# A streaming-encoder block in f32: ten 8 KB tiles instead of nine, 22 slots of 4 KB instead of 24, and another place for the eight value pieces

## The chip, the cores and the metric

The kernel runs on one core of one Trainium2 chip. The metric is the device time of one execution in microseconds (us). The kernel before takes 2405.63 us, the median of three runs (2405.38 to 2405.67).

The engines go by the names of the profile: PE (TensorE, matmuls and transposes), DVE (VectorE), ACT (ScalarE), POOL (GpSimd) and SP (SyncE). Each works through its own queue of instructions in order. SP does nothing but start loads. POOL starts other DMAs, among them those that add to what they write.

## The reference

One layer of an encoder block over 256 tokens with 2048 features, in float32, with 256 memory tokens:

```python
x = x + 0.5 * swiglu(rms_norm(x, ffn1_norm), ffn1_w_up, ffn1_w_down)   # d_ff = 5632

h = rms_norm(x, mix_norm)
proj = h @ w_in                                  # 6144 + 4096 columns
q_a, f_a, i_a, g_a, x_b, gate_b, gates = jnp.split(proj, splits, axis=-1)
o_a = hgrn2_chunked(q_a, f_a, i_a, lb)           # 8 heads of 128; i_a are the values
y_a = rms_norm(o_a, hgrn_norm) * silu(g_a)
y_b = rglru_branch(x_b, gate_b, conv_w, conv_b, lru_wa, lru_ba, lru_wx, lru_bx, lru_lambda)
g = sigmoid(gates + b_gate)
x = x + (g[A] * (y_a @ w_branch_a) + g[B] * (y_b @ w_branch_b)) @ w_out

q, k, v = rms_norm(x, xattn_norm) @ wq, *split(rms_norm(mem, mem_norm) @ wkv)   # 4 heads of 512
x = x + (softmax(q @ k.T / sqrt(512)) @ v) @ wo

x = x + 0.5 * swiglu(rms_norm(x, ffn2_norm), ffn2_w_up, ffn2_w_down)
return rms_norm(x, final_norm)
```

## The kernel before

**Numbers in two parts.** Every weight comes from HBM in pieces of 128 x 2048 f32, 1 MB or 8 KB in each partition. ACT rounds a piece to PE's faster type, which gives `h`; DVE subtracts `h` from the raw piece, which gives the remainder `l` (function `split`, L556: ACT `h<-raw`, DVE `l<-raw,h`). Activations are split in the same way: `ops` (the operands of the projections, the high and the low part side by side in one tile), `xf`, `xh` and `xl` (x as it enters the feed-forwards), `hidop` (the hidden layer). PE makes three of the four products, high by high, high by low and low by high, into one PSUM bank `acc`.

**Four kinds of pieces** (function `prepare`, L664). A *plain* piece is a load (`raw`), one `h` and one `l`. A *fast* piece belongs to a product that is made with seven sub-products instead of eight, and needs sums of its quarters besides: DVE makes three differences into the tile `td`, and `td` is split as well, into `th` and `tl`. A *value* piece (kind `"seven"`, the weights `wv` of the values `i_a`) is of the same sort; its operands on the other side are sums of quarters of the activations, made by DVE in slots `xs` (function `sums_of`) and split into slots `xd`. A *made* piece has its sums worked out long ahead, between the two feed-forwards: POOL loads the weights into a tile `made` (`made<-wu`), DVE makes the differences in place (`made<-made`), POOL writes the tile out to DRAM (`kept<-made`), and in the second feed-forward SP loads it back (`td<-kept`). Besides these, an *added* piece has its `l` made by DMAs on POOL, in tiles `own` and `l`.

**Two rings of tiles in SBUF.** All tiles of 8 KB (`raw`, `h`, `l`, `td`, `tl`, `made`, `own` and others, function `big`) share one ring: nine places in the whole program, and four more within each feed-forward (`FFN_POOLS = dict(more=4)`, L836). The tiles of 4 KB (function `slot`) share a ring of 24: halves of the sums (`th`), `xs`, `xd`, `ops`, the silu, gate and score tiles, the biases of the gates (`bgate`), the probabilities and values of the attention. A tile can be written when the last reader of the tile that had its place before is through.

**The stages.** The head takes the memory's norm and its values (weights `wvm`) between the first pieces of the first feed-forward; the residual x comes twice, as `xin` (by tokens, tiles `x`) and as `xT` (by features, eight parts of 128 x 512 into the tile `xf`). Then come the first feed-forward (weights `wu`, `wd`), the projections `win` (40 pieces, one bank each) with the eight value pieces among the first twelve, the two recurrences as side work between the projections, the gates (`wg`, 32 pieces in eight groups; for each two groups one load of biases `bgate` on SP), the branches, the output, the attention (per head: scores, a softmax whose probabilities are `p`, transposes `acc<-vt,p` on PE), and the second feed-forward, which ends with the last norm (`to_out`). Each projection is 16 matmuls of 512 columns with `h` (`acc<-ops,h` or `acc<-h,ops`, by which operand is the stationary one) and 16 of 256 columns with `l` (`acc<-ops,l`); then ACT copies half of the bank (`lo`), and DVE adds and scales (`sum`, `silu`). Each value piece is 21 matmuls of 512 columns into seven banks, which stay open from the first value piece to the last. There are eight banks.

**Where the value pieces stand.** The program's units of work for the first half are four `unit_f`, four `unit_silu(Q)` and four `unit_silu(G)`, twelve projections. Entry `a` of a list of eight numbers puts one value piece ahead of projection number `a` (numbered from 0; 12 is the end). The list stands twice for the weights' plan and once for the units:

```python
after = [2, 4, 5, 7, 8, 9, 11, 12]
more = [f for n in range(13) for f in [lambda: next(vs)] * after.count(n) + more[n:n + 1]] + [lambda: next(vs)]
```

**What sets the order.** The code doesn't issue its instructions directly. Each call is recorded (`Flow.record`, L220), and at the end a planner (`Flow.arrange`, L286) simulates the five queues with prices of its own (`Flow.price`), gives each operation a due time from the PE work that needs it (`aims`), and takes for each queue, of the operations whose inputs are ready, the one that is due first, if the ring has a place. So the number of places in a ring decides how far ahead a load or a `split` may be put. For the shared ring, the place is refused while earlier-due operations still lack theirs; for the slots, `fit` keeps a number of places spare, set by `3 if bufs == 24 else ...` (L173). The order is then written out by one loop (L488, which is why almost all rows of the profile show L488), with the semaphores that the order needs. All of PE's 11579 matmuls and transposes and all other operations are the same whatever the order; what differs is which stands ahead of which.

Of the kernel before, what the change touches and what calls it, by code (L numbers as in the profile page):

```python
# [80 lines left out]
class View:  # L81


    def __init__(self, tile, cells, steps=()):
        self.tile, self.cells, self.steps = tile, cells, steps
# [77 lines left out]
class Pool:  # L163
# [5 lines left out]
    def tile(self, shape, dt, name, tag=None, bufs=None):  # L169
        tag = tag or name  # L170
        if tag not in self.rings:
            bufs = bufs or self.bufs
            self.rings[tag] = Ring(tag, 3 if bufs == 24 else bufs // 4 if bufs >= 8 else bufs)  # L173
            self.rings[tag].extend(self, bufs)
        return Buffer(self.rings[tag], shape, dt, name, self.scope, "space" in self.kw)

# [23 lines left out]
class Flow:  # L200
# [22 lines left out]
    def pool(self, name, bufs, scope=None, **kw):  # L223
        self.pools.append(Pool(self, name, bufs, scope, **kw))
        return self.pools[-1]
# [267 lines left out]
def block_kernel(tc: tile.TileContext, xT, xin, memT, mem, vec, gfin, bgate, lruw, wu1, wd1, win, wv,  # L493
                 wg, wab, wout, wq, wk, wvm, wo, wu2, wd2, out_):
    flow = Flow(tc)
    pe, dve, act, sp, gps = flow.queues
    pool = flow.pool

    const = pool("const", 1)
    flow.share("big", pool("big", 9), 9)  # L500

    def big(name, dt=F32R):
        return flow.shared("big", [P, 2048], dt, name)

    slots = pool("slots", 24)
    small = pool("small", 2)
    dram = pool("dram", 1, space=bass.MemoryType.DRAM)
    psum = pool("psum", 8, space=bass.MemoryType.PSUM)
# [70 lines left out]
    def plan_columns(name, w, which):  # L579
        plan.extend(((name, i), w[i], "plain") for i in which)  # L580
# [6 lines left out]
    for hf in range(2):  # L587
        order = [*range(8 + hf * 4, 12 + hf * 4), *range(hf * 4, hf * 4 + 4), *range(16 + hf * 4, 20 + hf * 4)]
        for n, i in enumerate(order):
            for p, a in enumerate([2, 4, 5, 7, 8, 9, 11, 12] if hf == 0 else ()):  # L590
                if a == n:
                    plan.append((("v", "seven", p), wv[p], "seven"))
            plan_columns("in", win, [i])
        for p, a in enumerate([2, 4, 5, 7, 8, 9, 11, 12] if hf == 0 else ()):
            if a == 12:
                plan.append((("v", "seven", p), wv[p], "seven"))
    for hf in range(2):
# [285 lines left out]
    def turned_half(tile, y):  # L883

        acc = bank()
        for m in (2 * y, 2 * y + 1):
            for t in range(2):
                pe.transpose(acc[:, m % 2 * T + t * P:][:, :P], tile[:, t * 512 + m * P:][:, :P], ident)
        return acc
# [422 lines left out]
    def unit_silu(to, base, i):  # L1312
        hf, h = divmod(i, 4)
        if h == 0:
            to[hf] = slot(name="silu")
        s = summed(proj(base + i), by=rs["f"])
        o = heads(to[hf])[:, h]
        act.activation(o, s, ACT.Sigmoid)
        dve.tensor_tensor(out=o, in0=o, in1=s, op=ALU.mult)

    def unit_f(i):
        hf, h = divmod(i, 4)
        if h == 0:
            F[hf] = slot(name="f")
        s = summed(proj(8 + i), by=rs["f"])
        o = heads(F[hf])[:, h]
        act.activation(s, s, ACT.Sigmoid)
        dve.tensor_scalar(out=o, in0=s, scalar1=oml[:, i:i + 1], scalar2=lb[:, i:i + 1], op0=ALU.mult, op1=ALU.add)
# [9 lines left out]
    def units_v():  # L1338
        both = Halves()

        def sums(p):
            return sums_of([xg2[p // 2][:, p % 2 * 512 + j * P:][:, :P] for j in range(4)], both.new("xs"))

        accs = {}
        yield from seven("v", xs, sums, accs)
        joined(accs, [v[t][:, c * 512:(c + 1) * 512] for t in range(2) for c in range(2)])
        for t in range(2):
            act.activation(v[t], v[t], ACT.Copy, scale=rs["t"][:, t:t + 1])
        yield
# [171 lines left out]
    for hf in range(2):  # L1521
        more = [lambda i=i: unit_f(i) for i in range(hf * 4, hf * 4 + 4)]
        more += [lambda i=i: unit_silu(Q, 0, i) for i in range(hf * 4, hf * 4 + 4)]
        more += [lambda i=i: unit_silu(G, 16, i) for i in range(hf * 4, hf * 4 + 4)]
        if hf == 0:
            vs = units_v()
            after = [2, 4, 5, 7, 8, 9, 11, 12]
            more = [f for n in range(13) for f in [lambda: next(vs)] * after.count(n) + more[n:n + 1]] + [lambda: next(vs)]
        units += more
        units += [lambda hf=hf: side.append(hgrn(hf)) or True]  # L1530
# [291 lines left out]
```

## Time and profile before

| | |
|---|---|
| median of three runs | 2405.63 us (2405.38 to 2405.67) |
| the profiled execution | 2406.53 us, span in the profile 2404.8 us |
| busy: PE, DVE, ACT, POOL | 2392.7 (99%), 2128.1 (88%), 1473.3 (61%), 91.8 (4%) us |
| granted TensorE clock, mean | 0.999 |
| HBM | 581.12 MB read, 62.91 MB written, 268 GB/s over the span |

The profile was taken in one execution of its own, 0.90 us longer than the median of the runs; its span leaves out 1.7 us around the instructions. A row of a wait (`PE acc L488 <- DVE p L488: 1.4, 1, 1.4`) names the engine that stood still, the tile it was to write, who released it, the sum of the idle time in us, how often, and the longest. A row of the timeline gives the start in us, the time busy, the engine and the group of instructions, and in brackets the idle time just before with its releaser. In a row of windows stand, for one stretch, the busy time and the number of instructions of PE, PEld, DVE, ACT and POOL, then the granted clock, the busy share of the DMA engines and GB/s. In a row of instruction groups stand the busy time in us and the mean of one in ns, then the idle time of the engine in front of them. `x` and a number behind a group is how many instructions it holds; the names of x's tiles end in numbers (`x_304`).

### The profile page before, as it was taken

How to read it: one execution, taken by the hardware profiler on the slowest of the kernel's cores; microseconds unless marked ns; L12 is line 12 of the kernel's file. 1: busy time of each engine (PE TensorE's matmuls, PEld its weight loads, DVE VectorE, ACT ScalarE, POOL GpSimd, SP SyncE). 2: the span in 40 equal slices, each digit the busy share in tenths (PEclk: the TensorE clock that was granted, in tenths of full speed). 3: DMA queues.
4: the chain of work that ended last, by engine and by line, in shares of the span. 5: the costliest groups of instructions: out<-in, count | busy, mean ns of one | idle time of the engine just before them, and what ended most of it. 6: DMA issues, size and time to landing. Idle time of an engine off the chain costs nothing. (4 is left out here: it accounts for less than half of the span.)

```text
span 2404.8 us, 31100 instructions
## 1 busy us (share of the span) xinstructions
PE 2392.7 (99%) x12078; PEld 2000.9 (83%) x12078; DVE 2128.1 (88%) x2350; ACT 1473.3 (61%) x1470; POOL 91.8 (4%) x153
## 2 busy tenths in 40 slices
PE   9999999999999999999999999999999999999998
PEld 8888888888888888888888888888888888888887
DVE  7899999999996999888977788878799999999995
ACT  8767666666676655435773354555676666666663
POOL 0000000000000000000000000000000000000000
PEclk9999999999999999999999999999999999999999
DMA  9677788877776688889889899886898777777763
GB/s 370 238 261 243 258 261 263 262 256 253 260 252 204 224 321 297 322 306 347 315 312 338 316 371 363 305 303 248 309 378 319 262 262 262 263 262 262 259 265 114
DMA packets 101813, 678.58 MB, mean 282 GB/s; under 512 B 11296, under 2 KB 12064, under 8 KB 27296
## 3 DMA queue, kind: packets, MB, share of 16 engines
q1 hardware_dynamic: 79776, 523.40, 57.9%
q0 software_dynamic: 21168, 152.05, 20.1%
q8 instruction: 95, 1.56, 0.2%
q10 hardware_dynamic: 720, 1.13, 0.1%
q14 instruction: 54, 0.44, 0.1%
HBM read 581.12 MB, written 62.91 MB: 268 GB/s over the span
## 5 line engine op out<-in xcount | busy, mean ns | idle before, releaser
L488 DVE TENSOR_TENSOR l<-raw,h 128x2048 fp32r<-128x2048 f32 (+2 forms) x421 | 846.7, 2013 | 135.7 <-ACT h L488 62.3
L488 ACT ACTIVATE h<-raw 128x2048 fp32r<-128x2048 f32 (+2 forms) x421 | 711.1, 1693 | 391.5 <-PE acc L488 176.9
L488 PE MATMUL acc<-h,xh 128*128 128x512 f32 x1238 | 481.7, 390 | 0.3 <-DVE ev L488 0.3
L488 PE MATMUL acc<-h,xl 128*128 128x512 f32 x1238 | 481.6, 389 | 0.0
L488 ACT ACTIVATE h<-td 128x1024 fp32r<-128x1024 f32 (+1 forms) x264 | 326.0, 1241 | 200.3 <-DVE td L488 163.5
L488 DVE TENSOR_TENSOR tl<-td,h 128x1024 fp32r<-128x1024 f32 (+1 forms) x264 | 378.4, 1446 | 7.8 <-ACT h L488 4.0
L488 PE MATMUL acc<-h,hidop 128*128 128x512 f32 x1408 | 356.0, 390 | 0.0
L488 PE MATMUL acc<-h,ops 128*128 128x512 f32 x1312 | 315.5, 391 | 0.0
L488 PEld LDWEIGHTS acc<-h,hidop 128*128 128x128 f32 x1408 | 262.9, 188 | 53.8
L488 PEld LDWEIGHTS acc<-h,ops 128*128 128x128 f32 x1312 | 244.3, 188 | 49.8
L488 PE MATMUL acc<-ops,h 128*128 128x512 f32 x1152 | 285.0, 393 | 0.6 <-DVE ops L488 0.5
L488 PEld LDWEIGHTS acc<-h,xh 128*128 128x128 f32 x1238 | 232.4, 188 | 50.5 <-DVE ev L488 0.7
L488 PEld LDWEIGHTS acc<-h,xl 128*128 128x128 f32 x1238 | 232.4, 188 | 47.7
L488 PEld LDWEIGHTS acc<-ops,h 128*128 128x128 f32 x1152 | 211.7, 188 | 43.2 <-DVE sum L488 0.9
L488 PE MATMUL acc<-l,hidop 128*128 128x512 f32 x704 | 193.6, 389 | 0.0
L488 PE MATMUL acc<-tl,xh 128*128 128x512 f32 x640 | 176.2, 391 | 0.1
L488 PE MATMUL acc<-l,xh 128*128 128x512 f32 x598 | 166.0, 390 | 0.4 <-DVE l L488 0.4
L488 DVE TENSOR_TENSOR made<-made 128x512 f32<-128x512 f32 x224 | 153.1, 687 | 13.6 <-DMA made<-wu 10.3
L488 PE MATMUL acc<-l,ops 128*128 128x512 f32 x656 | 163.1, 389 | 0.0
L488 PEld LDWEIGHTS acc<-ops,l 128*128 128x128 f32 x1152 | 150.5, 191 | 6.6
L488 PEld LDWEIGHTS acc<-l,hidop 128*128 128x128 f32 x704 | 132.1, 188 | 27.6
L488 DVE TENSOR_TENSOR td<-raw,td 128x512 f32<-128x512 f32 x224 | 153.5, 685 | 0.7
(187 smaller groups left out, 2266.1 us busy)
## 6 DMA issues: line engine op xcount, KB each, us to landing
raw<-wu SPq DMA_DIRECT2D x109, 1024.0 KB, 5.9
raw<-wd SPq DMA_DIRECT2D x68, 1024.0 KB, 5.5
made<-wu POOLq DMA_DIRECT2D x56, 1024.0 KB, 7.3
kept<-made POOLq DMA_DIRECT2D x56, 1024.0 KB, 8.1
td<-kept SPq DMA_DIRECT2D x56, 1024.0 KB, 6.7
raw<-wu SPq DMA_DIRECT2D x56, 768.0 KB, 4.9
raw<-win SPq DMA_DIRECT2D x40, 1024.0 KB, 6.4
raw<-wg SPq DMA_DIRECT2D x32, 1024.0 KB, 7.5
```

What stands on the lines that cost most here:

```text
L488: getattr(op.queue.real, method)(*map(real, args), **{k: real(v) for k, v in kw.items()})
```

## The change

The shared ring of 8 KB tiles gets ten places instead of nine (so 14 instead of 13 in each feed-forward), the ring of 4 KB slots 22 instead of 24, which is the same memory. The number that recognises the slot ring in L173 follows, so that its spare places stay three. The value pieces stand ahead of the projections 1, 3, 4, 6, 7, 9, 10 and 11 instead of 2, 4, 5, 7, 8, 9, 11 and behind the last.

```diff
--- before.py
+++ after.py
@@ -170,7 +170,7 @@
         tag = tag or name
         if tag not in self.rings:
             bufs = bufs or self.bufs
-            self.rings[tag] = Ring(tag, 3 if bufs == 24 else bufs // 4 if bufs >= 8 else bufs)
+            self.rings[tag] = Ring(tag, 3 if bufs == 22 else bufs // 4 if bufs >= 8 else bufs)
             self.rings[tag].extend(self, bufs)
         return Buffer(self.rings[tag], shape, dt, name, self.scope, "space" in self.kw)
 
@@ -497,12 +497,12 @@
     pool = flow.pool
 
     const = pool("const", 1)
-    flow.share("big", pool("big", 9), 9)
+    flow.share("big", pool("big", 10), 10)
 
     def big(name, dt=F32R):
         return flow.shared("big", [P, 2048], dt, name)
 
-    slots = pool("slots", 24)
+    slots = pool("slots", 22)
     small = pool("small", 2)
     dram = pool("dram", 1, space=bass.MemoryType.DRAM)
     psum = pool("psum", 8, space=bass.MemoryType.PSUM)
@@ -587,11 +587,11 @@
     for hf in range(2):
         order = [*range(8 + hf * 4, 12 + hf * 4), *range(hf * 4, hf * 4 + 4), *range(16 + hf * 4, 20 + hf * 4)]
         for n, i in enumerate(order):
-            for p, a in enumerate([2, 4, 5, 7, 8, 9, 11, 12] if hf == 0 else ()):
+            for p, a in enumerate([1, 3, 4, 6, 7, 9, 10, 11] if hf == 0 else ()):
                 if a == n:
                     plan.append((("v", "seven", p), wv[p], "seven"))
             plan_columns("in", win, [i])
-        for p, a in enumerate([2, 4, 5, 7, 8, 9, 11, 12] if hf == 0 else ()):
+        for p, a in enumerate([1, 3, 4, 6, 7, 9, 10, 11] if hf == 0 else ()):
             if a == 12:
                 plan.append((("v", "seven", p), wv[p], "seven"))
     for hf in range(2):
@@ -1524,7 +1524,7 @@
         more += [lambda i=i: unit_silu(G, 16, i) for i in range(hf * 4, hf * 4 + 4)]
         if hf == 0:
             vs = units_v()
-            after = [2, 4, 5, 7, 8, 9, 11, 12]
+            after = [1, 3, 4, 6, 7, 9, 10, 11]
             more = [f for n in range(13) for f in [lambda: next(vs)] * after.count(n) + more[n:n + 1]] + [lambda: next(vs)]
         units += more
         units += [lambda hf=hf: side.append(hgrn(hf)) or True]
```

No operation is added or removed. By both lists the first value piece and the last have ten projections between them. Three places in the order of the instructions show what the planner makes of it. The names stand in the form output<-inputs with the size; `x` and a number is a run of equal rows.

*SP, the first loads.* These are loads into the tiles of x (`x` from `xin`, `xf` from `xT`), of the memory (`memory`), of the constants (`vt`) and of weights (`raw`). Before:

```order
L488 DMA xf<-xT 128x512 x3
L488 DMA raw<-wvm 128x2048 x2
L488 DMA x_266<-xin 128x512
L488 DMA raw<-wvm 128x2048
L488 DMA x_293<-xin 128x512
L488 DMA x_299<-xin 128x512
L488 DMA x_304<-xin 128x512
L488 DMA xf<-xT 128x512 x5
L488 DMA raw<-wvm 128x2048
L488 DMA vt<-vec 128x240
L488 DMA raw<-wvm 128x2048
L488 DMA memory<-mem 128x2048
```

After:

```order
L488 DMA xf<-xT 128x512
L488 DMA raw<-wvm 128x2048
L488 DMA xf<-xT 128x512 x6
L488 DMA raw<-wvm 128x2048
L488 DMA memory<-mem 128x2048
L488 DMA raw<-wu 128x2048
L488 DMA memory<-mem 128x2048
L488 DMA xf<-xT 128x512
L488 DMA vt<-vec 128x240
```

Counted from the start of SP's queue, the last of the eight `xf` loads stood behind six loads of whole weight pieces (1 MB each), and now stands behind nine of them and both loads of `memory`, five loads of 1 MB more.

*PE, from the end of the first feed-forward into the projections.* `x_304` is the last part of the new x, turned by transposes (`acc<-vt,x_304`); `ops,h` and `ops,l` are projections, `diag,ones` carries the norm's factor to the features, and `h,ops`, `h,xd`, `th,xd`, `l,ops`, `l,xd` are value pieces. Before:

```order
L488 MATMUL acc<-ops,h 128x512 x10
L488 MATMUL acc<-vt,x_304 128x128 x8
L488 MATMUL acc<-ops,h 128x512 x2
L488 MATMUL acc<-ops,l 128x256 x12
L488 MATMUL acc<-ops,h 128x512 x7
L488 MATMUL acc<-diag,ones 128x256
L488 MATMUL acc<-ops,h 128x512 x5
L488 MATMUL acc<-ops,l 128x256 x4
L488 MATMUL acc<-ops,h 128x512 x8
L488 MATMUL acc<-ops,l 128x256 x16
L488 MATMUL acc<-h,ops 128x512 x4
L488 MATMUL acc<-h,xd 128x512 x2
```

After:

```order
L488 MATMUL acc<-ops,h 128x512 x10
L488 MATMUL acc<-vt,x_304 128x128 x8
L488 MATMUL acc<-ops,h 128x512 x2
L488 MATMUL acc<-ops,l 128x256 x12
L488 MATMUL acc<-h,ops 128x512 x3
L488 MATMUL acc<-ops,h 128x512 x2
L488 MATMUL acc<-h,ops 128x512
L488 MATMUL acc<-h,xd 128x512 x2
L488 MATMUL acc<-th,xd 128x512 x4
L488 MATMUL acc<-l,ops 128x512 x2
L488 MATMUL acc<-l,xd 128x512
```

Before, the first value piece follows behind two whole projections; now its first matmuls stand right behind the first projection's first 12 `ops,l`, and some of them ahead of the second projection's `ops,h`.

*PE, the first softmax of the attention.* `acc<-vt,p` are the transposes of the probabilities `p` of one head. Before:

```order
L488 MATMUL acc<-ops,h 128x512 x16
L488 MATMUL acc<-ops,l 128x256 x16
L488 MATMUL acc<-ops,h 128x512 x7
L488 MATMUL acc<-vt,p 128x128 x4
L488 MATMUL acc<-ops,h 128x512 x9
```

After:

```order
L488 MATMUL acc<-ops,h 128x512 x16
L488 MATMUL acc<-ops,l 128x256 x16
L488 MATMUL acc<-ops,h 128x512 x15
L488 MATMUL acc<-vt,p 128x128 x4
L488 MATMUL acc<-ops,h 128x512
```

The four transposes now stand behind 15 instead of 7 matmuls of the projection under way. On DVE, one `l` and one `ops` more stand ahead of that head's `p`, and two `made<-made` fewer.

Elsewhere: on SP the loads of the pieces of `win` and `wv` alternate as before, with one `win` instead of two ahead of the first `wv`. The third load of `bgate` stands behind 21 loads of `wg` instead of 15, and the fourth behind all 32 instead of 26. ACT changes its function table 26 times instead of 27.

## The prediction

> **What bounds the kernel now.** I read the page first (busy time and the granted clock), then the waits of PE, the timeline of PE, the chain that ended last.
>
> ```profile
> span 2404.8 us, 31100 instructions
> PE 2392.7 (99%) x12078; PEld 2000.9 (83%) x12078; DVE 2128.1 (88%) x2350; ACT 1473.3 (61%) x1470; POOL 91.8 (4%) x153
> ...
> PEclk9999999999999999999999999999999999999999
> ```
>
> PE (TensorE) is idle for 2404.8 − 2392.7 = 12.1 us only, at full clock throughout. The waits of PE and its last long piece in the chain tell where these lie:
>
> ```profile
> PE acc L488 <- DVE p L488: 1.4, 1, 1.4
> PE warm L488 <- DVE ones L488: 1.1, 1, 1.1
> PE acc L488 <- DVE ops L488: 0.5, 1, 0.5
> PE acc L488 <- DVE l L488: 0.4, 1, 0.4
> PE acc L488 <- DVE ev L488: 0.3, 1, 0.3
> ...
> 1966.17 430.70 PE acc L488 x1927
> ```
>
> The start costs 1.1 us, and after PE's end at 1966.17 + 430.70 = 2396.87 come 2404.8 − 2396.9 = 7.9 us of final norm and store, which the change doesn't touch. That leaves 12.1 − 1.1 − 7.9 = 3.1 us of visible idle time in the middle. A busy PE is not the whole truth, since records overlap:
>
> ```profile
> 753.04 2.20 PE L488 MATMUL acc<-h,hidop 128*128 128x512 f32 x9
> 755.08 0.39 PE L488 MATMUL acc<-l,hidop 128*128 128x512 f32 x1
> ```
>
> Nine matmuls of 512 columns start in 755.08 − 753.04 = 2.04 us, one each 0.227 us, while a record lasts 0.39: a wait shows only beyond 0.39 − 0.227 = 0.16 us. With five or ten such hidden remainders the middle holds 4 to 5 us that any change of buffers could win. The number of matmuls, and of PE's switches between matmuls and transposes, is the same in both programs, so all that can change is waiting.
>
> **The change part by part.** Durations are of the profiled execution (span 2404.8 us, its own time 2406.53); the median of the runs is 2405.63, 0.90 us less. Terms are differences, so I apply them to the median.
>
> *The attention (the largest wait).* POOL, DVE and PE in the timeline:
>
> ```profile
> 1563.23 0.54 POOL L488 DMA_DIRECT2D made<-wu  x1 [6.62 <-DMA kept<-made]
> ...
> 1574.08 1.29 DVE L488 TENSOR_TENSOR made<-made 128x512 f32<-128x512 f32 x2 [2.06 <-DMA made<-wu]
> ...
> 1583.02 0.27 PE L488 MATMUL acc<-vt,p 128*128 128x128 f32 x1
> ...
> 1584.73 0.55 PE L488 MATMUL acc<-vt,p 128*128 128x128 f32 x3 [1.44 <-DVE p L488]
> ```
>
> The load of a `made` tile waited 6.62 us for its place in the ring, until an earlier `kept` had been written out; it landed late; DVE stood 2.06 us in front of it with the softmax of a head queued behind; PE then waited 1.44 us for that softmax. In the new order eight more projection matmuls stand ahead of these transposes (7 become 15), which is 8 × 0.227 = 1.8 us more cover, and the ring has one more place. DVE gets some work there as well (an `l` of 2.29 and a short `ops` against two `made` of 0.69: +1.3 us). If the late load stays late, the wait is 1.44 + 1.3 − 1.8 = 0.9; if it isn't late, nothing. I take nothing: −1.4 us (bounds −1.4 and 0), because the wait for the place is what a tenth place answers.
>
> *The value pieces.* The rows of their start, and DVE's groups of 780 to 960 us:
>
> ```profile
> 783.59 1.42 PE L488 MATMUL acc<-ops,h 128*128 128x512 f32 x5 [0.45 <-DVE ops L488]
> ...
> 788.79 2.07 PE L488 MATMUL acc<-ops,l 128*128 128x256 f32 x16
> 790.69 1.09 PE L488 MATMUL acc<-h,ops 128*128 128x512 f32 x4
> ```
>
> ```profile
> L488 DVE TENSOR_TENSOR l<-raw,h 128x2048 fp32r<-128x2048 f32 x25 | 57.1, 2286 | 2.8 <-ACT h L488 1.8 <-PE acc L488 1.0
> ...
> L488 DVE TENSOR_TENSOR tl<-td,th 128x1024 fp32r<-128x1024 f32 x16 | 19.0, 1220 | 1.1 <-PE acc L488 1.0
> L488 DVE TENSOR_TENSOR l<-raw,h 128x1536 fp32r<-128x1536 f32 x8 | 14.0, 1751 | 0.0
> L488 DVE TENSOR_TENSOR td<-raw,td 128x512 f32<-128x512 f32 x16 | 10.9, 683 | 0.0
> L488 DVE TENSOR_TENSOR td<-raw 128x1024 f32<-128x1024 f32 x8 | 9.7, 1217 | 0.0
> L488 DVE TENSOR_TENSOR sum<-acc,lo 128x256 f32<-128x256 f32 x23 | 9.6, 419 | 0.0
> L488 DVE TENSOR_TENSOR sum<-sum,rstd 128x256 f32<-128x256 f32 x23 | 9.0, 418 | 0.0
> L488 DVE TENSOR_TENSOR silu<-silu,sum 128x256 f32<-128x256 f32 x15 | 6.2, 418 | 0.0
> ...
> L488 DVE TENSOR_TENSOR xd<-xs,xd 128x512 fp32r<-128x512 f32 x7 | 4.8, 684 | 0.0
> L488 DVE TENSOR_TENSOR xs<-xg 128x128 f32<-128x128 f32 x14 | 4.0, 285 | 0.0
> ```
>
> By busy time per instruction, a value piece costs DVE 1.21 + 2 × 0.68 + 1.75 + 2 × 1.19 + 4 × 0.29 + 0.69 = 8.5 us, and PE 21 × 0.227 = 4.8: it eats 3.7 us of lead. A projection costs DVE 2.28 + 0.42 + 0.39 + 0.41 = 3.5 and PE 16 × 0.227 + 16 × 0.119 (1.90 / 16, from 788.79 to 790.69) = 5.5: it gives 2.0 back. Before and after, ten projections stand between the first and the last value piece, and the worst run is three pieces in consecutive projections, 3 × 3.7 − 2 × 2.0 = 7.1 us of lead. So the new spread is no more even; it only starts one projection earlier, with 2.0 us less lead, against which the tenth tile lets DVE stand one `l` (2.29 us) further ahead. Term: +2.0 − 2.3, about 0; bounds −0.2 (the short waits there go) and +2.0 (the tile gives no lead). At the start matmuls of the value piece now stand where PE waited 0.45 us for the last `ops`: −0.45, but the first piece's operands are wanted after some 24 matmuls instead of two whole projections, about 8 us sooner, by engines that have no time laid by; I take the same 0.45 for a new wait, so 0 (bounds −0.45 and +1.8, what the nearest unhidden lateness, DVE's 2.06, would show).
>
> *The head.* Windows, the first matmul on x, the waiting one, and the loads of x (tile `xf`):
>
> ```profile
> 50.00:100.00 50.00, 50.00 (x222) 41.24 (x221) 37.81 (x50) 42.83 (x53) 2.62 (x4) 1.00 0.78 272
> 100.00:110.00 10.00, 10.00 (x46) 8.17 (x45) 10.00 (x11) 5.89 (x5) 0.00 (x0) 1.00 0.59 211
> ...
> 72.62 0.39 PE L488 MATMUL acc<-h,xh 128*128 128x512 f32 x1
> ...
> 110.93 0.97 PE L488 MATMUL acc<-l,xh 128*128 128x512 f32 x3 [0.36 <-DVE l L488]
> ...
> L488 SPq DMA_DIRECT2D xf<-xT x8: 328/328/432, 23.4 to 41.4; - x8
> ...
> DMA to landing us min/median/max: 5.2/7.8/9.2
> ```
>
> With more tiles the planner loads weights earlier and x later: five more loads of 1 MB now stand ahead of the last `xf`. At 272 GB/s that is up to 5 × 3.9 = 19 us, so it is issued by 61 and lands by 70, ahead even of the first matmul on x (72.62); it is the last of eight parts. Hidden by 3 us there and by more for that part. The conversion work moves behind 50 us, where DVE has 50 − 37.8 = 12.2 us free; if that cover were gone it would meet the stretch from 100 us, where DVE is full and PE already waits 0.36. A "fast" weight piece there costs DVE about 1.22 + 2 × 0.68 + 1.75 + 2 × 1.22 = 6.8 against PE's 4.8. Bounds −0.4 and +2.0 (one such deficit unpaid); I take +0.4, the present wait once more.
>
> *The start of the second feed-forward.*
>
> ```profile
> 1750.00:1800.00 50.00, 49.67 (x221) 39.93 (x220) 47.58 (x32) 35.67 (x25) 0.00 (x0) 1.00 0.94 369
> ...
> 1770.13 0.50 PE L488 MATMUL acc<-h,xh 128*128 128x512 f32 x1 [0.30 <-DVE ev L488]
> ```
>
> 0.33 us idle, DVE nearly full. One tile further ahead takes it: −0.3 (bounds −0.3, +0.4). In the long stages of both feed-forwards nothing idles, and 14 tiles for 13 changes nothing: 0.
>
> *Two slots fewer.* Slots ran to 24 only around the recurrences, gates and scores. The load that pays is `bgate`:
>
> ```profile
> DMA to landing us min/median/max: 4.6/7.3/10.3
> ...
> L488 SPq DMA_DIRECT2D raw<-wg x32: 327/328/412, 1036.9 to 1224.1; - x32
> ...
> 1242.25 1.40 DVE L488 SCALAR_TENSOR_TENSOR gate<-acc,rtok,bgate 128x512 f32<-128x512 f32 x2
> ```
>
> The last `bgate` now stands behind all 32 loads of `wg`. These ended at 1224.1, and its first use is at 1242.25: landing takes 10.3 at worst, so 7.9 us of cover, more with a tenth tile. Term 0; without that cover DVE, whose queue is in order, would stop with a pair of banks and every `l` behind it, 1 us of PE for each us late.
>
> Sum: −1.4 + 0 + 0 + 0.4 − 0.3 + 0 = −1.3, so 2405.63 − 1.3 = 2404.3 us, 0.05% less: no change by the bound of 0.2% (4.8 us), which is about what a measurement can tell here.
>
> **The rivals.**
>
> A: every wait in the middle was a lack of places. For it speaks the 6.62 us row; against it that `ops`, `l` and `ev` waited for DVE's own work. All visible ones gone: 2405.63 − 3.1 = 2402.5. [...]
>
> B (slower): a value piece's operands come late at the new start, the lead is not regained before the run of three, and PE pays its 7.1 us: 2412.7. It decides when the tile adds less than the 2.0 us lost and the old lead was under 5 us. Against it: before, PE lost only 0.15 us from 850 to 900 in such a run. [...]
>
> C (slower): slots block. `bgate` or a slot of the scores comes 5 us beyond its cover: 2411.
>
> D: the new order only swaps its waits for others as long: 2405.6 ± 1.
>
> **How the numbers follow.** Forecast 0.62 (own range 2402.9 to 2406.3), A 0.07, D 0.16, B 0.10, C 0.05. Predicted 2404.3. The range leaves out most of B and C and the hidden remainders beyond A: 2402.2 to 2409.5; its upper end is the sum of the upper bounds less one of them (0 + 2.0 + 1.8 + 2.0 + 0.4 = 6.2, less 2.0, is +4.2, to 2409.8). Faster by over 0.2% (below 2400.8) would need more than all waits in the middle: 0.02. Slower (above 2410.4): B, nearly all, and C: 0.14. The rest, 0.84, within.
>
> **What would show it.** PE busy again 2392 to 2393 us with the same 12078 records; no wait on `p` over 1 us; DVE's waits for `made<-wu` shorter; the wait at the end of the first feed-forward group of 0.4 to 0.9; none on `bgate`. I am wrong if PE's idle time in the middle grows past 5 us: a wait on `h`, `tl` or `xd` between 780 and 900 would mean B, one on a gate or score tile C, one on `xh` before 110 that x came too late.

## The result, and the profile after

The changed kernel takes 2410.76 us (median of 12 runs, 2409.70 to 2411.62), the kernel before 2405.44 us over the runs beside it: 5.3 us or 0.22% more, ratio 1.0021 with the 95% interval 1.0014 to 1.0029. That is slower beyond the spread of the runs; whether it is more than the prediction's bound of 0.2%, the interval leaves open. It lies beyond the range that was given (2402.2 to 2409.5). The profiled execution after has a span of 2409.0 us, 4.2 more than before. The page after:

```profile
span 2409.0 us, 31062 instructions
PE 2394.0 (99%) x12078; PEld 2000.8 (83%) x12078; DVE 2131.0 (88%) x2350; ACT 1472.2 (61%) x1469; POOL 91.8 (4%) x153
...
PEclk9999999999999999999999999999999999999999
```

The records (12078) and the clock are those of before, so I read all that is new as waiting. Not all of it shows as idle time: PE's busy time itself grew by 1.3 us (2392.7 to 2394.0), and since records overlap (0.39 us each, one every 0.227), waits of up to 0.16 us hide in it, as the prediction worked out. That these make up the 1.3 us is likely, but no row shows them one by one. PE's waits after (sum in us, how often, the longest):

```profile
PE acc L488 <- DVE ops L488: 1.7, 2, 1.4
PE acc L488 <- DVE l L488: 1.6, 2, 1.1
PE acc L488 <- DVE p L488: 1.3, 1, 1.3
PE warm L488 <- DVE ones L488: 1.1, 1, 1.1
PE acc L488 <- ACT h L488: 0.8, 2, 0.5
PE acc L488 <- DVE tl L488: 0.3, 2, 0.2
PE acc L488 <- ACT ops L488: 0.3, 1, 0.3
```

By the prediction's reckoning the middle holds 2409.0 − 2394.0 − 1.1 − 7.9 = 6.0 us of visible idle time, where it held 3.1. To see in which stage, I take the starts of rows that mark stages in both timelines of PE: the first projection, the first transpose of the merged branches, the first score, the first matmul of the second feed-forward. Before:

```profile
777.48 0.84 PE L488 MATMUL acc<-ops,h 128*128 128x512 f32 x3
...
1274.64 0.60 PE L488 MATMUL acc<-vt,merge 128*128 128x128 f32 x4
...
1540.92 0.52 PE L488 MATMUL acc<-ops 128*128 128x512 f32 x2
...
1724.74 0.39 PE L488 MATMUL acc<-h,xh 128*128 128x512 f32 x1
```

After:

```profile
777.49 0.84 PE L488 MATMUL acc<-ops,h 128*128 128x512 f32 x3
...
1277.02 0.60 PE L488 MATMUL acc<-vt,merge 128*128 128x128 f32 x4
...
1543.07 0.40 PE L488 MATMUL acc<-ops 128*128 128x512 f32 x1
...
1728.16 0.39 PE L488 MATMUL acc<-h,xh 128*128 128x512 f32 x1
```

PE's end before is that of the prediction's last row (2396.87). After, PE's last long piece in the chain ends at 2021.24 + 379.89 = 2401.13:

```profile
2021.24 379.89 PE acc L488 x1699
```

The projections with the value pieces, recurrences and gates took 1274.64 − 777.48 = 497.16 us and take 499.53 (+2.4); from the branches to the scores nothing is lost (−0.2); the attention with its output took 183.82 and takes 185.09 (+1.3); the second feed-forward, up to PE's end, took 672.13 and takes 672.97 (+0.8). The head and the first feed-forward together are level (777.48 and 777.49). So the whole loss lies in the three places for which the prediction had terms of 0, −1.4 and −0.3. I read all further kernels by the same four rows and PE's end. Where kernels have the same order in a stage, its length differs by up to 0.4 us from one execution to another (the projections of the change, e4 and e10 below: 499.53, 499.69 and 499.44; the second feed-forward of the change, e4 and e10: 672.97, 673.30 and 672.93), so I read nothing into less.

### The profile page after: what moved, and what is told of

Same layout as the page of the kernel before. It is cut to its first block, busy times and chain, and to the rows that moved or that the text cites. A ratio compares the mean times of both kernels' runs of the same rounds, so it can differ in the third digit from the quotient of the medians.

```text
span 2409.0 us, 31062 instructions
## 1 busy us (share of the span) xinstructions
PE 2394.0 (99%) x12078; PEld 2000.8 (83%) x12078; DVE 2131.0 (88%) x2350; ACT 1472.2 (61%) x1469; POOL 91.8 (4%) x153
## 5 line engine op out<-in xcount | busy, mean ns | idle before, releaser
L488 PE MATMUL acc<-h,xh 128*128 128x512 f32 x1238 | 474.6, 390 | 0.6 <-ACT h L488 0.5
L488 PE MATMUL acc<-h,xl 128*128 128x512 f32 x1238 | 474.2, 389 | 0.0
```

Of the source, the lines that this page charges most:

```text
L488: getattr(op.queue.real, method)(*map(real, args), **{k: real(v) for k, v in kw.items()})
```

## The experiments

**The two parts apart.** Theory 1 was that each part has its own price; theory 2 that the rings make all of it; theory 3 that no part has a price, since any edit lets the planner write another order.

```diff
 # e1: rings as before, the new places for the value pieces
-after = [2, 4, 5, 7, 8, 9, 11, 12]
+after = [1, 3, 4, 6, 7, 9, 10, 11]
 # e2: the new rings, the old places
-flow.share("big", pool("big", 9), 9)
+flow.share("big", pool("big", 10), 10)
-slots = pool("slots", 24)
+slots = pool("slots", 22)
 # e3: nine tiles, the old places, 22 slots (and the spare three with them)
-slots = pool("slots", 24)
+slots = pool("slots", 22)
```

> Nine tiles and 24 slots as before, the value pieces in their new places. Theory 1 (the parts add: the new places cost the waits of the value stretch, the rings those of the attention and of the second feed-forward): PE waits 1 to 1.5 us for an operand of a value piece between 780 and 900 us, the attention keeps the wait of 1.4 us on p that it had before, and the kernel takes 2405.4 + 1.7 = 2407 us. Theory 2 (the rings make all of it): 2405.4, no new wait. Theory 3 (no part has a price of its own; any edit lets the planner write another order, with waits wherever a ring or an engine happens to be short): the difference from before and that of the rings alone don't add up to the whole change's 5.3 us, within 1.5 us.

> Ten tiles and 22 slots, the value pieces in their old places. Theory 1: no wait over 0.6 us between 780 and 900 us; the two waits of 1.3 and 1.4 us in the attention (on p near 1611 and on ops near 1628) and that on l near 1894 are there; 2405.4 + 1.7 + 0.9 + 0.1 = 2408 us. Theory 2: 2410.8. Theory 3: a sum with the first kernel that isn't the whole change's, and waits in the value stretch at other places.

> Nine tiles, 22 slots, the value pieces in their old places. By the prediction's term for two slots fewer (0): 2405.4, within 1 us, and the same waits as before. If the slots are what the attention lacks: waits on ops or p between 1540 and 1650 us that are longer by 1.5 us or more in sum than before, 2407 or above.

Measured, with the stages' lengths against before, in us:

| kernel | median | ratio, 95% interval | projections | attention | second feed-forward |
|---|---|---|---|---|---|
| the change | 2410.76 | 1.0021 (1.0014 to 1.0029) | +2.4 | +1.3 | +0.8 |
| e1, positions only | 2408.71 | 1.0012 (1.0004 to 1.0021) | +2.7 | −1.2 | 0.0 |
| e2, rings only | 2411.33 | 1.0027 (1.0016 to 1.0038) | +2.7 | +0.3 | +0.7 |
| e3, slots only | 2404.91 | 0.9997 (0.9988 to 1.0006) | +0.3 | −2.5 | 0.0 |

The parts don't add. By the medians the positions alone cost 3.0 us and the rings alone 5.6 (against 2405.71 beside them), 8.6 together, and the whole change 5.3; with intervals of 1 to 5, 4 to 9 and 3 to 7 us that alone would prove little. The stages are clearer: in the projections each part alone costs 2.7 us and both together 2.4. The edit of the positions, which doesn't touch the attention, shortens it by 1.2 us, through the order alone. (Another 0.9 us of e1's profiled execution lies ahead of the projections, where PE waited 0.60 us for a first load at 12.88 us; the last section comes back to that.) Two slots fewer cost nothing: the attention lost its wait on `p` and 2.5 us, and the kernel is level with before. Theories 1 and 2 fall; theory 3 is what they leave, but the attention below limits it too.

What the rings alone do to the projections (e2), on PE, and on DVE just ahead of the first of these waits:

```profile
866.09 3.92 PE L488 MATMUL acc<-ops,h 128*128 128x512 f32 x16 [0.87 <-DVE sum L488]
893.23 0.74 PE L488 MATMUL acc<-silu,k 128*32 128x16 f32 x64 [1.32 <-DVE silu L488]
894.52 3.94 PE L488 MATMUL acc<-ops,h 128*128 128x512 f32 x16 [0.56 <-ACT h L488]
```

```profile
857.94 3.22 DVE L488 TENSOR_TENSOR made<-made 128x512 f32<-128x512 f32 x5
...
862.28 2.29 DVE L488 TENSOR_TENSOR l<-raw,h 128x2048 fp32r<-128x2048 f32 x1
864.48 1.22 DVE L488 TENSOR_TENSOR td<-raw 128x1024 f32<-128x1024 f32 x1
865.62 0.42 DVE L488 TENSOR_TENSOR sum<-acc,lo 128x256 f32<-128x256 f32 x1
```

A short `sum` for which PE waited stood behind five `made<-made`, an `l` and a `td`. With the tenth place, `made` tiles come in earlier. The sums on `made` tiles from 780 to 860 us (the columns are busy time and number on DVE and on POOL, the clock, the DMA share and GB/s), before the change and in e2:

```profile
780.00:860.00 80.00, 4.65 (x7) 2.20 (x4) 1.00 0.66 239
```

```profile
780.00:860.00 80.00, 6.18 (x10) 2.20 (x4) 1.00 0.62 237
```

Ten sums instead of seven begin before 860 us; nine in the changed kernel. But e1, with nine places, has eight there and loses as much in the projections as e2, so early sums alone don't explain the loss. DVE has no time to spare there, before the change (49.3 of 50 us from 800 to 850) or after. The same window of the changed kernel (DVE's is the third busy time):

```profile
800.00:850.00 50.00, 50.00 (x266) 43.08 (x265) 48.82 (x75) 29.28 (x33) 2.20 (x4) 1.00 0.64 243
```

This gave the next two theories for the value stretch: that it is the order in DVE's queue (optional work ahead of wanted work), or that the stretch is short of DVE's time and of places, whoever stands first.

**Putting the optional work behind, in e2.** The planner's order is kept, and nine sums on DVE are moved (rows of DVE's order):

```diff
-made<-made x5, xs<-xg, made<-made, xs, xs
+made<-made x2, xs<-xg, xs, xs
 l<-raw,h
 td<-raw
 sum<-acc,lo
+made<-made x4
 ...
-made<-made x3, td<-raw, made<-made
+td<-raw
 ...
-made<-made
 ...
 silu<-silu,f
+made<-made x5
```

> The kernel with ten tiles, 22 slots and the old positions (2411.3), with DVE's order mended at two places of the value stretch: four made sums that stood ahead of a sum near 862 go behind it, and five that stood ahead of a silu between 875 and 889 go behind that. Order theory (the waits come from optional work that stands ahead of wanted work in DVE's queue): the waits of 0.9 us on sum (866) and 1.3 us on silu (893) both go, and nothing of over 0.5 us comes in their place: 2411.3 - 2.2 = 2409.1. Shortage theory (the stretch has no DVE time or no places left, whoever stands first): the postponed sums hold their tiles longer, and at least 1.5 us come back before 1000 us as waits on l, h, tl or xd: 2410.5 or above.

Measured: 2420.41 us, ratio 1.0062 (1.0049 to 1.0074), 9.1 us more than e2. The order theory falls for this stretch, hard. The chain in the trace, from POOL to PE, begins with the postponed sums' write:

```profile
868.13 0.54 POOL L488 DMA_DIRECT2D kept<-made  x1 [2.82 <-DVE made L488]
...
876.47 7.28 SPq L488 DMA_DIRECT2D raw<-win  x2
...
886.23 1.91 ACT L488 ACTIVATE h<-raw 128x2048 fp32r<-128x2048 f32 x1 [6.81 <-DMA raw<-win]
888.04 0.36 ACT L488 ACTIVATE lo<-acc 128x256 f32<-128x256 f32 x1
...
888.44 0.42 DVE L488 TENSOR_TENSOR sum<-acc,lo 128x256 f32<-128x256 f32 x1 [4.51 <-ACT lo L488]
...
888.92 2.50 PE L488 MATMUL acc<-ops,h 128*128 128x512 f32 x5 [3.50 <-DVE sum L488]
```

In e2 that write was issued at 862.36 and the load at 868.30. In e5 SP's queue stood 10.3 us for a `kept<-made` ahead of this load: the load takes the place of a `made` tile that is being written out. So the write 5.8 us later made the load 8.2 us later; `h` on ACT waited for it with a wanted `lo` queued behind; DVE waited for `lo`, and PE for `sum`. Of the 9.1 us, 3.5 are this wait and some 1.6 the slower clock behind it (last section); two more waits that e2 doesn't have are 1.15 us on `th` at 873 and 1.88 on `l` at 907. A sum on a `made` tile isn't optional: its tile's place is promised to a load.

**One write, one tile less.** Two kernels take a `made` tile's hold away instead.

```diff
 # e6: the changed kernel, one write left out
-kept<-made            (POOL, 841 us)
 # e9: e2 without the second made tile
-made<-wu              (POOL)
-made<-made x4         (DVE, 859 to 862 us)
-kept<-made            (POOL)
```

> The changed kernel without one write: the first made tile's sums aren't written to DRAM (the second feed-forward reads another piece's sums in their place), and all else keeps its order. PE's wait of 1.12 us on l near 852 follows a DVE wait of 0.75 us for a place that this write held from 841 to 850. If the write's hold on the place makes the wait: it falls below 0.5 us, since l's input was there at 846.1, and the kernel takes 2410.8 - 0.9 = 2409.9. If it is DVE's time (the value pieces' rate, rival B of the prediction): DVE's 0.75 us go, PE's wait stays above 0.7 us, and the time within 0.4 us of 2410.8.

> The kernel with ten tiles, 22 slots and the old positions (2411.3) without one made tile: the second one's load, its four sums (859 to 862 us, ahead of a sum that PE waited for) and its write are left out, and the second feed-forward reads another piece's sums in their place; all else keeps its order. Theory: with the tenth place a made tile comes into the value stretch earlier than before (ten of its sums lie before 860 us, seven before the change), and its DVE time (2.8 us) and its place are what the stretch lacks: the waits on sum near 866 (0.87 us) and on silu near 893 (1.3 us) go, 2411.3 - 2.2 = 2409.1. Rival: the waits belong to the value pieces themselves, and at least 1.5 of the 2.7 us that the projections take longer stay: 2410.5 or above.

e6 addresses the largest wait of the changed kernel in this stretch. The write on POOL, `l` on DVE and the wait on PE, in the changed kernel:

```profile
841.30 0.54 POOL L488 DMA_DIRECT2D kept<-made  x1 [2.38 <-DMA raw<-wv]
...
850.63 1.76 DVE L488 TENSOR_TENSOR l<-raw,h 128x1536 fp32r<-128x1536 f32 x1 [0.75 <-DMA kept<-made]
...
852.44 0.74 PE L488 MATMUL acc<-l,ops 128*128 128x512 f32 x2 [1.12 <-DVE l L488]
```

The same in e6, where DVE's row has no wait in front:

```profile
850.04 1.75 DVE L488 TENSOR_TENSOR l<-raw,h 128x1536 fp32r<-128x1536 f32 x1
...
851.84 0.73 PE L488 MATMUL acc<-l,ops 128*128 128x512 f32 x2 [0.28 <-DVE l L488]
```

The wait falls from 1.12 to 0.28 and the projections become 0.8 us shorter, as expected if the write's hold on the place makes the wait. The kernel takes 2409.93 us (ratio 1.0019, 1.0010 to 1.0029), the time expected, though such intervals can't tell 0.8 us. The 0.28 us stay although DVE no longer stands still ahead of its `l`; I put them down to DVE's time. In e9 the wait of 0.87 us on `sum` is gone, that of 1.32 on `silu` stays, the projections are 1.1 us shorter than in e2 (+1.5 against before), and the time is 2409.82 us (1.0018, 1.0009 to 1.0027), 1.5 less than e2 and between the two expectations. So the earlier `made` tile costs about 1.1 of the 2.7 us, and the rest isn't its. Its load, sums and write went together, so e9 doesn't part its place from its time on DVE.

**Start, spread, and the feed-forwards' tiles.** Is it the earlier start that costs the lead (rival B of the prediction), or the spread? And does the middle's order stand by itself?

```diff
 # e11: ten tiles, 22 slots, the old start, no three pieces in consecutive projections
-after = [1, 3, 4, 6, 7, 9, 10, 11]
+after = [2, 3, 5, 6, 8, 9, 11, 12]
 # e12: the changed kernel, 13 tiles in the feed-forwards as before
-FFN_POOLS = dict(more=4)
+FFN_POOLS = dict(more=3)
```

> Ten tiles and 22 slots as in the changed kernel, the value pieces ahead of the projections 2, 3, 5, 6, 8, 9, 11 and behind the last: the old start, and no three of them in consecutive projections. If the early start costs the lead (rival B): no wait on an operand of a value piece before 860 us, the projections as long as before within 0.5 us, and 2405.4 + 0.3 + 0.7 + 0.4 = 2407 us (attention, second feed-forward and the part ahead of the scores as with the rings alone). If neither start nor spread sets it, but the order that the planner happens to find: the projections longer by 1.5 to 3 us, as in every kernel so far that changed rings or positions, 2409 or above.

> The changed kernel with three added tiles instead of four in each feed-forward, so that both have 13 as before and only the stages between have ten. If the fourteenth tile makes what the second feed-forward loses (0.8 us from its first x matmul to PE's end) and what the head swaps (a wait of 0.5 us on h at 91 for one of 0.4 on l at 111): both are as before, the projections (+2.4) and the attention (+1.3) stay as in the changed kernel, and 2410.8 - 0.8 = 2410.0 us. If the order of the middle hangs on the feed-forwards' too: the projections' or the attention's length changes by 1 us or more.

e11 takes 2408.84 us (1.0015, 1.0006 to 1.0024), with projections longer by 1.8 us: neither the start nor the spread sets the loss by itself, and PE waits for a `tl` of value pieces at 874 and 886 us:

```profile
874.51 0.50 PE L488 MATMUL acc<-tl,xd 128*128 128x512 f32 x1 [0.35 <-DVE tl L488]
...
886.65 0.50 PE L488 MATMUL acc<-tl,xd 128*128 128x512 f32 x1 [0.48 <-DVE tl L488]
```

e12 takes 2412.96 us (1.0032, 1.0020 to 1.0044). The second feed-forward loses 0.3 us instead of 0.8. Over all kernels here the two groups don't overlap: those with 14 tiles in it lose 0.7 to 1.2 us there, those with 13 (e1, e3, e7, e12) −0.1 to 0.3. So the fourteenth tile makes this loss, or most of it. The head has its old wait near 111 back. But the projections, whose code and rings are those of the changed kernel, are longer by 4.4 us instead of 2.4: what the planner does in the first feed-forward shifts the order of everything behind it. Twelve sums on `made` tiles stand before 860 us there.

**One tile less.** If the tenth tile brings nothing, are tiles not short at all?

```diff
-flow.share("big", pool("big", 9), 9)
+flow.share("big", pool("big", 8), 8)
-slots = pool("slots", 24)
+slots = pool("slots", 26)
```

> The rings changed the other way, eight tiles and 26 slots, the value pieces in their old places. If tiles were short, one less costs more than ten tiles gave or took: the value stretch and the attention lose 4 us or more, 2410 or above, and every long wait is one for a place. If the number of tiles only draws another order: somewhere from 2403 to 2412 us, as with ten tiles, with waits at other places.

Measured: 2439.11 us, ratio 1.0137 (1.0123 to 1.0151), 33 us more: +7.0 up to the first projection, +13.3 in the projections, +9.1 from the branches to the scores, −1.0 in the attention, +3.9 in the second feed-forward. The waits on operands come back in number:

```profile
PE acc L488 <- ACT h L488: 10.2, 8, 3.6
PE acc L488 <- DVE k L488: 3.2, 1, 3.2
PE acc L488 <- DVE merge L488: 2.0, 2, 1.8
```

Eight tiles are short, then. Nine are enough but for single waits, and a tenth brought no more in any order tried. Of the eight waits on `h` here, three come between 86 and 114 us and five later. With nine tiles, where each wait comes once, there was little left to win.

**The attention.** Of the changed kernel, POOL's load, DVE and PE around the two waits:

```profile
1600.14 0.54 POOL L488 DMA_DIRECT2D made<-wu  x1 [8.35 <-PE acc L488]
...
1609.48 0.69 DVE L488 TENSOR_TENSOR made<-made 128x512 f32<-128x512 f32 x1 [2.20 <-DMA made<-wu]
...
1611.22 0.55 PE L488 MATMUL acc<-vt,p 128*128 128x128 f32 x3 [1.34 <-DVE p L488]
...
1621.38 2.29 DVE L488 TENSOR_TENSOR l<-raw,h 128x2048 fp32r<-128x2048 f32 x1 [4.23 <-PE acc L488]
...
1625.17 2.29 DVE L488 TENSOR_TENSOR l<-raw,h 128x2048 fp32r<-128x2048 f32 x1
1627.38 0.76 DVE L488 TENSOR_TENSOR ops<-sum,ops 128x256 fp32r<-128x256 f32 x2
...
1627.85 1.68 PE L488 MATMUL acc<-ops 128*128 128x512 f32 x8 [1.42 <-DVE ops L488]
```

The first is the wait of before in another place: a load into a `made` tile is late, DVE stands in front of it, and a softmax is queued behind. Only what held up the load differs: before, a `kept` that was being written out (the prediction's row at 1563.23), here a tile that PE was still reading. In the second, an `l` waits 4.23 us for its tile, and short `ops` that PE wants stand behind it and a second `l`. e4 moves the four sums behind the softmax and the second `l` behind the `ops`; e10 leaves that `made` tile out.

```diff
 # e4, DVE
-made<-made, st<-st, made<-made, p<-p,st, made<-made, sum, sum, made<-made, ps, ops
+st<-st, p<-p,st, sum, sum, ps, ops, made<-made x4
 ...
-l<-raw,h, ops<-sum,ops x2
+ops<-sum,ops x2, l<-raw,h
 # e10
-made<-wu, made<-made x4, kept<-made      (1600 to 1614 us)
```

> The changed kernel with two places of DVE's order mended: the four made sums for whose load DVE stood 2.2 us in front of a softmax near 1609 go behind that softmax, and one l that stood ahead of two short ops near 1625 goes behind them; nothing else moves. If it is DVE's order (late or long work ahead of short work that PE waits for) that makes the two waits, both go, 1.3 + 1.4 us, and nothing takes their place: 2410.8 - 2.7 = 2408.1 us. If a shortage stands behind them (of slots, tiles or DVE's time), the waits come back within 50 us, on p, ops or l, and the time stays within 1 us of 2410.8.

> The changed kernel without the made tile for whose load DVE stood 2.2 us in front of a softmax near 1609: load, four sums and write left out (the second feed-forward reads another piece's sums in their place), all else in its order. If the late load is the cause: the wait of 1.3 us on p near 1611 goes, that of 1.4 us on ops near 1628 stays (an l ahead of it waits for its tile), none comes near 1635 as it did when the sums were only moved: 2410.8 - 1.3 = 2409.5. If the attention is short of DVE's time: a wait on p or ops of over 0.8 us stays or comes instead, and both waits together lose less than 0.7 us.

e4 takes 2409.33 us (1.0017, 1.0009 to 1.0026): both waits are gone, but a new one has come, so that the attention is 1.7 us shorter and not 2.7. On PE in e4:

```profile
1634.81 0.55 PE L488 MATMUL acc<-vt,p 128*128 128x128 f32 x3 [1.05 <-DVE p L488]
```

e10 takes 2409.32 us (1.0016, 1.0007 to 1.0025): the wait on `p` is gone, that on `ops` stays at 1.4, and none comes near 1635. The attention is 2.1 us shorter, some 0.3 to 0.5 of it by a wait on `ops` at 1546 (0.30 in the changed kernel), ahead of the edit, that this execution doesn't show. So the late `made` load is the cause of the wait on `p`. As that on `ops` stays in e10, it was the other move, of the `l`, that took it in e4. That e4's new wait comes of the 2.8 us of DVE time that the moved sums still take is likely but not shown, since e10 doesn't have the moved `l` either.

Both waits stand in every kernel with ten places in which I left this stretch alone: in e2, e5, e6, e9, e11 and e12 that on `p` takes 0.9 to 1.5 us, and that on `ops` 1.42 in each. With nine places PE waits in the attention for one `p` at most (1.44 us before, 0.94 in e1, none in e3 and e7) and not for `ops`. So here the ten places bring the same two waits each time, with a stage that is 0.3 to 1.3 us longer than before, and that isn't a new draw.

**Mending the best order.** The kernel with 22 slots and nothing else changed was the quickest so far, so I mended the three places in it where PE still waited.

```diff
 # DVE, 110 us
-td<-raw,td, l<-raw,h
+l<-raw,h, td<-raw,td
 # ACT, 782 us
-xg<-acc,vt x3, ops<-xg, xg<-acc,vt
+xg<-acc,vt x2, ops<-xg, xg<-acc,vt x2
 # DVE, 861 us
-made<-made x2, l<-raw,h, xd<-xs,xd, sum<-acc,lo
+l<-raw,h, xd<-xs,xd, sum<-acc,lo, made<-made x2
```

> The kernel with nine tiles, 22 slots and the old positions (2404.9), with three places of the order mended: near 110 us a td of 0.7 us goes behind the l that PE waits for, near 782 us an xg on ACT behind the ops that PE waits for, near 861 us two made sums behind the sum that PE waits for. Order theory: the waits there (0.38, 0.46 and 0.15 us) fall by 0.35 us each or to nothing, together 0.8 us: 2404.1. Shortage theory: the waits only move on, 2404.9 within 0.3 us.

Measured: 2406.03 us, ratio 1.0001 (0.9992 to 1.0010), no gain; the profiled span is 1.3 us longer than that of e3. The wait at 110 us moved to an `h` at 112 (0.31 us), the one on `ops` at 783 stayed (0.46), and in place of the 0.15 on `sum` near 865 came one on `th`:

```profile
884.52 0.73 PE L488 MATMUL acc<-th,xd 128*128 128x512 f32 x2 [0.59 <-ACT th L488]
```

The projections are 1.4 us longer than in e3, where only an `xg` and two `made` sums were put later in that stretch: as in e5, the wait that they had made was the cheaper one. None of the kernels beats the kernel before clearly; e3's 2404.91 us is level with it.

## Why the prediction was wrong

*What bounds the kernel.* Right: the matmuls, their number and the clock didn't change, and the difference is waiting, 2.9 us of it visible and 1.3 us, as far as can be told, inside PE's busy time. Of the signs named beforehand three failed: PE is busy 2394.0 us and not 2392 to 2393, there is a wait of 1.34 on `p`, and the idle time in the middle, 6.0 us, is past 5.

*The attention, −1.4.* The wait of 1.44 on `p` went, as forecast, and over the whole kernel DVE's waits for `made` loads fell from 10.3 us (eight times) to 2.5 (twice): what the tenth place was to answer, it answered. The step that failed is that nothing else was counted: "if the late load stays late" was asked of that one load. In the new order one of the two late loads that were left stood ahead of another softmax, for 1.3 us (e10), and an `l` without a place held up `ops` for 1.4. The stage measured +1.3, where the bounds were −1.4 and 0: a miss of 2.7 us, the largest of all terms. The slots weren't it (e3: −2.5 with the same 22).

*The value pieces, 0.* It measured +2.4, the second largest miss. "The tenth tile lets DVE stand one `l` further ahead" (−2.3) is the step that failed: no order with ten places is quicker in the projections. In every order with ten places, two to five more sums on `made` tiles stand before 860 us than before the change (e2, e11: 10, changed: 9, e12: 12, against 7), so that a part of the tile's worth goes into work that nobody waits for yet, and that then holds its place until it has been written out (e6: 0.8 us of the wait at 852) and takes DVE's time (e9: 1.1 us for both). That is not the whole cause, since e1 loses 2.7 with nine places. The price of the start, +2.0 at most by the prediction, was near those 2.7 that the positions alone cost; but e11 has the old start and loses 1.8 with ten tiles, so the loss doesn't need the new start. Right at the start the term held: waits of 0.25 on `ops` at 784 and 0.27 on `h` at 790 stand for the one of 0.45.

*The head, +0.4.* The wait on `l` at 111 went and one of 0.55 on `h` at 91 came; up to the first projection the profiled executions are level, 0.0. Right in its bounds, 0.4 below the term.

*The second feed-forward, −0.3.* The wait on `ev` at 1770 went. Then "in the long stages nothing idles, and 14 tiles for 13 changes nothing" failed: new waits on `l` (0.52 us at 1894) and `tl` make +0.8, which kernels with 13 tiles there don't lose.

*Two slots fewer, 0.* Right (e3), and `bgate` made no wait. The cover was thinner than it seemed: of the four loads of `bgate` one took 16.6 us to land, where the prediction had 10.3 as the worst.

*The range.* The upper bounds add to +6.2 us, and the loss of 5.3 would lie within that. The range left one bound of 2.0 out and was set to end at 2409.5, where its own sum gave 2409.8. And the loss came in part where the bounds allowed none, in the attention.

*The rivals.* B named the stretch that lost most, but not its size (2.4 for 7.1) and only in part its cause; of the waits on `h`, `tl` or `xd` that were to show it, only that of 0.27 came, and the long one was on `l`. D, the exchange of waits, is nearest to what happened; its fault is the ±1. I took the exchange to be even, and it was not: of five orders with ten tiles that the planner itself wrote or nearly so (the change, e2, e11, e12, and e9 with a tile left out), all lost, 1.5 to 4.4 us in the projections. The sum was made from the waits that the profile of before shows. The profile showed what the edit would take away, but not what another order would bring, and here, where DVE is busy 49 of 50 us, the second was the larger number.

The profiled executions account for +4.2 of the 5.3 us between the medians; the profiled execution of before took 2406.53, 1.1 above its median. What stays open is why no order with ten tiles that I tried is as good as that of before, and whether the order of before is simply a lucky one: of two others with nine places, e3 is as good and e1 isn't. In the projections a place held too long is shown for 0.8 us in the changed kernel (e6), and an early `made` tile for 1.1 in the one with the rings alone (e9); the rest of the loss there has no shown cause. A kernel in which `made` tiles can't use the tenth place wasn't tried.

## What to carry to other kernels

Where one program orders all queues, a change of a buffer count or a position can redraw the order in stages that it doesn't touch: price it as the spread that such edits show (here −1 to +8 us for e1, e2, e3, e11, e12 and the change), not by the one wait that it answers. Some of the price may still be systematic, as in the attention and the second feed-forward here, so compare several orders before calling it chance. Look at how a shared ring's extra place will be spent: here work that nobody waited for yet took a part of it, and kept it until its slowest reader was through, a DMA that landed 6 to 9 us after its issue (the `kept` writes of the changed kernel from 780 to 900 us). Work that holds a place someone else was promised is not optional, however late its result is wanted: put it late and the loss grows down every queue that is in order (in e5 a write 5.8 us later led to a load 8.2 us later and PE's wait of 3.5).

## What the runs showed that I had not expected

In e5 the longest wait cost more than its length: after PE's pause of 3.50 us at 888.92, nine matmuls took 3.5 us, one each 0.39 us for the usual 0.227. The granted clock of that window (behind PE, PEld, DVE, ACT and POOL), with the windows ahead and behind:

```profile
880.00:888.90 8.90, 5.42 (x32) 4.47 (x30) 2.88 (x5) 2.67 (x4) 0.00 (x0) 0.99 0.87 309
888.90:892.40 3.50, 3.48 (x9) 2.77 (x10) 3.50 (x3) 0.94 (x1) 0.00 (x0) 0.55 0.79 269
892.40:896.00 3.60, 3.60 (x20) 3.03 (x19) 2.36 (x6) 0.42 (x1) 0.00 (x0) 1.00 0.87 344
```

At a clock of 0.55 for 3.5 us, (1 − 0.55) × 3.5 = 1.6 us are lost on top of the pause, by estimate; with eight tiles the same follows a pause of 3.64 us at 1540.76, with a clock of 0.55 from 1540.7 to 1544.2. In the kernel with eight tiles the clock was also 0.50 from 916.5 to 919.8 us, at the end of a pause of 3.20 us, and from 878.9 to 882.2, behind one of only 1.84 us at 877.77, the last of five waits of over 0.5 us within 18 us; its mean over that execution is 0.997, where before it is 0.999. A pause of 1.88 us at 906.70 in e5 left it at 1.00. So in these two kernels the length of the last pause alone doesn't tell whether the clock falls. The waits of the changed kernel, 1.4 us at most, left the clock at full speed (1.00 behind the two longest, from 1611.22 to 1615.00 and from 1627.80 to 1631.50).

The first loads differed from one execution to the next. With the same order up to there, the changed kernel shows no wait near 13 us, and e6 shows this one, for a first piece of weights:

```profile
13.01 1.21 PE L488 MATMUL acc<-h,ms 128*128 128x512 f32 x4 [1.02 <-ACT h L488]
```

Little of it lasts: the next eight `acc<-l,ms` begin 0.5 us later in e6 than in the changed kernel (16.81 for 16.27), and the first projection 0.3 us (777.75 for 777.49). So some tenths of a microsecond of a single execution belong to no kernel, and stages are better compared by their lengths than by one run's end.
